# Storing the weight sums of one more feed-forward block, and making the sums in two parts around the latents

## The chip, the core and the metric

The kernel runs on one core of a Trainium2 chip. TensorE (PE) multiplies, VectorE (DVE) and ScalarE (ACT) work element by element, GpSimd (POOL) does small things and starts some transfers, SyncE (SP) starts the others. The metric is the time of one execution in microseconds on the device; the profile's span, from the first to the last instruction, is a little shorter.

## The reference

Two layers run over a stream of 256 tokens of 2048 numbers. Each layer mixes tokens and then applies a gated feed-forward network:

```python
for i in range(DEPTH):                      # 2
    mix = _hybrid_mixer(x, positions, w_in[i], g_cq[i], g_ckv[i], w_uq[i], w_ukv[i], w_o[i])
    x = _layer_norm(ALPHA * x + mix, ln1_g[i], ln1_b[i])
    h = silu(x @ w_gate[i]) * (x @ w_up[i])  # 2048 -> 5632
    x = _layer_norm(ALPHA * x + h @ w_down[i], ln2_g[i], ln2_b[i])
```

The mixer projects `x` with one matrix `w_in`. Its columns give queries, keys and values of sparse attention, an indexer that picks 64 keys for a query, and two latents (`cq`, `ckv`), which are normed by their root mean square and projected again (`w_uq`, `w_ukv`) for latent attention. All is float32.

## The kernel before

**Products in three passes.** A float32 weight tile of 128 x 1024 (a unit: 2 times 128 rows, 512 columns) is loaded as `raw`. ACT copies it to `wh`, rounded to the format that PE multiplies fast (L350), and DVE makes the rest `wl = raw - wh` (L351). `x` is held as a high and a low half too (`xhl`). A product of 128 x 128 by 128 x 512 is three matmuls: high by `wh`, high by `wl`, low by `wh` (L372 to L374, L690 to L692, L993 to L996, L1105 to L1107).

**A layer in order.** `proj` runs over the units of a block of `w_in`; the blocks come as QI0, TA (the indexer's key and weights, and most of `cq`), QI1, TB (the rest of `cq`, and `ckv`), KA0, then the latents' products (`w_uq`, `w_ukv`, in `mla_half` and `nope_T`), QA0, VA0 and so on, and the output projection with `w_o`. Behind TB, `tb_post` norms the latents, with POOL taking the power (L601, L603) and DVE scaling by it (L604). The feed-forward part has 11 blocks fc of 512 columns. Each has a gate and up part, here gu(fc), and hidden activations `hT`, which come in pairs into down parts, here d(fc), the one ahead of gu(fc).

**Quads.** From fc = 1 on gu(fc) goes by a scheme with seven products in place of eight. A quad takes units u and u + 4 of gate and of up for both halves of the tokens. A plain quad (N) has 8 passes over 4 loaded units, each 2 x 3 matmuls. A Strassen-Winograd quad (S) has 7 passes on 7 weight tiles: three are units, four are sums and differences of units that DVE makes on the spot (L1050, L1057, L1062, and a sum by an adding transfer, L329 and L330). It also needs four combinations of `x` for its unit, kept in `many` or `few`, made by `sum_operands` (L932, L937 and `split`). A made quad (Q) is the same with the four weight sums read from device memory, `ready[fc]`, where they were stored during attention. `ORDER` and `UNIT` say which quad runs where: NSSS for fc = 1, SSNS for 2 and 3, and SSQS from `ALLFROM` = 4 on, with unit `EARLY` = 0 for Q.

**Sets.** `presums` makes the stored sums. A set is one fc: four units are loaded on POOL's queue (L778) into `q`, four DVE operations make the sums (L789, L790, L792, L793), four transfers on POOL's queue store them (L798). `not_until_now` (L339) is a one-column POOL operation that writes into the new tile and reads the newest `wh`, so that the load can't start before the work has come so far; `gate` (L788) does the same for the sums. There are four `q` tiles, so that one set follows the other.

**What sets the order.** Side tasks such as `presums`, `indexer` and `mla_attend` are Python generators: `spawn` starts one, `yield n` lets n units of `proj` go by (`tick`), `finish` runs one to its end. That order of writing is the priority by which the framework fills each engine's queue ahead of the run, where it takes a later instruction into a gap if its inputs and a buffer are free. Each engine then works its queue in that order. Tiles with one tag share a fixed number of slots: `a8` has 10 of 8 KB a partition, for the two `x`, the four halves of the split `x`, `few`, `hT` and others, and a tile whose slot is taken waits for the last reader of an older one. `first_operands` makes the combinations for unit 0 in the down part ahead of fc = `ALLFROM`, behind the first column of its first `hT`.

Of the kernel before, what the change touches and what calls it, by code (L numbers as in the profile page):

```python
# [55 lines left out]
NFC = FFN // C  # L56
# [5 lines left out]
SOON = 200  # L62
FIRSTD = 2
T2, T2MORE = 4, 6
ALLFROM, EARLY = 4, 0


QI0, TA, QI1, TB, KA0, QA0, VA0, KA1, QA1, VA1 = range(10)
# [14 lines left out]
def hybrid_trunk(ctx: ExitStack, tc: tile.TileContext, x, xt_in, pos, w_in, g_cq, g_ckv, w_uq,  # L83
# [9 lines left out]
    def nm(s):  # L93
        uid[0] += 1
        return f"{s}{uid[0]}"
# [7 lines left out]
    def turn(name):  # L103
        if phase["cm"] is not None:
            phase["cm"].__exit__(None, None, None)
        phase["cm"] = None
        if name is not None:
            phase["cm"] = tc.tile_pool(name=nm(name), bufs=1)
            phase["pool"] = phase["cm"].__enter__()
        phase["name"] = name  # L110

    def pt(shape, dt, s, tag=None, bufs=1):
        assert phase["name"] == "att"
        return phase["pool"].tile(shape, dt, name=nm(s), tag=tag or s, bufs=bufs)

    def t4(shape, dt, s):
        return pt(shape, dt, s, "a4", 8)
# [33 lines left out]
    def f(ap):  # L151
        return ap.bitcast(F32)
# [22 lines left out]
    def load_x():  # L175
        for t in range(NT):
            nc.sync.dma_start(xt[t], x[t * P:(t + 1) * P, :])
# [105 lines left out]
    def step(task):  # L283
        try:
            task[0] = units_gone[0] + (next(task[1]) or 1)
        except StopIteration:
            tasks.remove(task)
# [7 lines left out]
    def spawn(gen):  # L295
        task = [0, gen]
        tasks.append(task)
        step(task)
        return task
# [5 lines left out]
    def finish(*ends):  # L305
        while any(e in tasks for e in ends):
            for task in list(tasks):
                if any(e in tasks for e in ends):
                    step(task)
# [25 lines left out]
    def not_until_now(*tiles):  # L335


        for v in tiles:
            nc.gpsimd.tensor_tensor(v[:, 0:1], mhalf, f(latest["wh"][:, 0:1]), op=ALU.add)  # L339
# [18 lines left out]
    def proj(units, lhs, n, before=None, split_t=None, banks=None):  # L358

        o = [bank(i, "acc") for i in banks] if banks else [acc() for _ in range(NT)]
        loaded = []
        last = len(units) - 1

        def go(t, u):
            (wh, wl), ks = loaded[u], units[u][1]
            for j, k in enumerate(ks):
                h, l = lhs(t, k)
                a, b = wh[:, j, :n], wl[:, j, :n]  # L370
                first, final = u == 0 and j == 0, u == last and j == len(ks) - 1
                mm(o[t][:, :n], h, a, start=first, stop=False)  # L372
                mm(o[t][:, :n], h, b, start=False, stop=False)  # L373
                mm(o[t][:, :n], l, a, start=False, stop=final)  # L374

        for u, (src, ks) in enumerate(units):
            if before is not None:
                before(u)
            loaded.append(load_unit(src, src.shape[-1]))
            for t in range(1 if split_t else NT):  # L380
                go(t, u)
            tick()
        if split_t:
            split_t()
            for u in range(len(units)):
                go(1, u)
                tick()
        return o
# [149 lines left out]
    def layer(l, xT, norms, last):  # L538
        xk = xlhs(xT)

        def in_chunk(b, before=None, split_t=None):
            n = IN_BLOCKS[b][1]
            return proj([(w_in[b][l, u], range(u * KU, (u + 1) * KU)) for u in range(NKT // KU)], xk, n,
                        before, split_t)
# [191 lines left out]
        def dsa_qk(b):  # L736
            dst = t4([P, 4, S], F32, "qk")
            o = in_chunk(b)
            return dst, spawn(heads_T(o, 4, A_DIM, A_ROT, [cosA[:, t] for t in range(NT)],
                                      [sinA[:, t] for t in range(NT)], dst))  # L740
# [26 lines left out]

        ready = {}

        def presums():  # L770

            for fc in range(ALLFROM, NFC):
                u = EARLY

                def load(i, v):
                    d = pt([P, KU * C], F32, "q", bufs=4)
                    not_until_now(d)
                    nc.gpsimd.dma_start(d, w_gu[i][l, fc, v])  # L778
                    return d

                b12, b22 = load(1, u), load(1, u + HALF)
                yield 1
                b11 = load(0, u)
                yield 1
                b21 = load(0, u + HALF)
                yield 4
                gate = pt([P, 1], F32, "gate", bufs=2)
                nc.gpsimd.tensor_tensor(gate, b12[:, 0:1], f(latest["wh"][:, 0:1]), op=ALU.add)  # L788
                nc.vector.tensor_tensor(b12, b12, b22, op=ALU.add)  # L789
                nc.vector.tensor_tensor(b11, b12, b11, op=ALU.add)  # L790
                yield 1
                nc.vector.tensor_tensor(b22, b11, b22, op=ALU.subtract)  # L792
                nc.vector.tensor_tensor(b21, b11, b21, op=ALU.add)  # L793
                yield 1
                ready[fc] = {}
                for i, (name, v) in enumerate((("p7", b12), ("p6", b11), ("p5", b22), ("p4", b21))):
                    d = hbm.tile([P, KU * C], F32, name=nm("q"), tag=f"{l}_{fc}_{name}", bufs=1)
                    nc.gpsimd.dma_start(d, v)  # L798
                    ready[fc][name] = d
                    if i % 2:  # L800
                        yield 1

        def aff(c):
            if l:
                affine(ln2_g[l - 1], ln2_b[l - 1], c)
# [20 lines left out]
        ckvT = t4([P, 2, KVL // P, S], F32R, "ckvT")  # L826
        qpT = t4([P, M_HEADS // 2, S], F32, "qpT")
        bias = [pt([P, P * (t + 1)], F32, f"selb{t}") for t in range(NT)]
        o = in_chunk(TA)
        aff(1)  # L830
        p_ta = spawn(ta_post(o))
# [6 lines left out]
        p_tb = spawn(tb_post(o))  # L838
        if l == 0:
            load_x()  # L840
        early = spawn(presums())
        ka, p_ka = dsa_qk(KA0)
        finish(p_tb)
        o = proj([(w_uq[2][l, u], range(u * KU, (u + 1) * KU)) for u in range(QL // P // KU)], cqk, C)
# [54 lines left out]
                        nc.vector.scalar_tensor_tensor(sl, o, by, sl, op0=ALU.mult, op1=ALU.add)  # L899
                then(t)  # L900

        finish(early)
        turn("more")
        gbT = load_gbT(ln1_T[l])
        xT, norms = [], []
# [241 lines left out]
        def finish_hidden():  # L1147
            finish(*[h[2] for h in held])

        ORDER = {1: "NSSS", 2: "SSNS", 3: "SSNS"}  # L1150
        UNIT = {"NSSS": (0, 2, 3, 1), "SSNS": (1, 2, 0, 3), "SSQS": (1, 2, EARLY, 3)}

        g = gu(0, 0, lambda: finish(*norms))
# [5 lines left out]
        for fc in range(1, NFC):  # L1159
            order = ORDER.get(fc, "SSQS")  # L1160
            if fc >= FIRSTD:
# [24 lines left out]
    for l in range(DEPTH):  # L1186
        xT, norms = layer(l, xT, norms, l == DEPTH - 1)
# [51 lines left out]
```

## Time and profile before

| | |
|---|---|
| time, median of 3 runs | 2145.45 us |
| lowest and highest | 2143.92 and 2145.48 us |
| time of the profiled execution | 2147.09 us |
| its span | 2145.3 us |
| granted TensorE clock, mean | 0.997 of 2.4 GHz |
| busy: PE, weight loads, DVE, ACT, POOL | 99%, 82%, 86%, 61%, 15% |
| read from and written to device memory | 503.37 MB and 31.46 MB |

Times of rows are counted from the start of the span. The first 20 us are start-up, about 20 to 434.8 us is attention and gate and up of block 0 in layer 0, and layer 1 begins near 1071. Matmuls are pipelined, and a matmul is listed with the time from its start to its modelled end, which overlaps the next. Releasers in brackets say what ended the idle time before an instruction.

### The profile page before, as it was taken

How to read it: one execution, taken by the hardware profiler on the slowest of the kernel's cores; microseconds unless marked ns; L12 is line 12 of the kernel's file. 1: busy time of each engine (PE TensorE's matmuls, PEld its weight loads, DVE VectorE, ACT ScalarE, POOL GpSimd, SP SyncE). 2: the span in 40 equal slices, each digit the busy share in tenths (PEclk: the TensorE clock that was granted, in tenths of full speed). 3: DMA queues.
4: the chain of work that ended last, by engine and by line, in shares of the span. 5: the costliest groups of instructions: out<-in, count | busy, mean ns of one | idle time of the engine just before them, and what ended most of it. 6: DMA issues, size and time to landing. Idle time of an engine off the chain costs nothing.

```text
span 2145.3 us, 28442 instructions
## 1 busy us (share of the span) xinstructions
PE 2129.4 (99%) x9946; PEld 1768.9 (82%) x9946; DVE 1850.9 (86%) x2343; ACT 1311.5 (61%) x1695; POOL 321.6 (15%) x514
## 2 busy tenths in 40 slices
PE   9999999999999999999999999999999999999997
PEld 7888888888888888888888888888888888888886
DVE  6697776899999999999867976678999999999997
ACT  5555554766566666766655555447666666666773
POOL 0122220021111100110013222201111111110111
PEclk9999999999999999999999999999999999999999
DMA  8677879588888899888657877885897888989984
GB/s 295 216 279 272 310 277 328 175 217 267 239 245 270 286 278 300 269 273 255 216 176 242 298 276 276 315 281 187 245 274 224 256 265 274 288 275 293 286 296 115
DMA packets 161905, 558.21 MB, mean 260 GB/s; under 512 B 18161, under 2 KB 18465, under 8 KB 161121
## 3 DMA queue, kind: packets, MB, share of 16 engines
q1 hardware_dynamic: 111168, 399.69, 52.2%
q0 software_dynamic: 50448, 156.57, 28.4%
q8 instruction: 78, 1.28, 0.2%
q14 instruction: 67, 0.54, 0.1%
q10 hardware_dynamic: 144, 0.13, 0.0%
HBM read 503.37 MB, written 31.46 MB: 249 GB/s over the span
## 4 chain that ended last, share of the span: by engine, by line
PE 86%; DVE 7%; issue 3%; DMA 2%; ACT 1%; POOL 0%; SPq 0%; POOLq 0%; DVEq 0%; ACTq 0%
PE acc L372 8%; PE acc L373 8%; PE acc L374 8%; PE acc L1106 7%; PE acc L1107 7%; PE acc L1105 7%; PE gu_p L996 6%; PE gu_p L993 6%; PE gu_p L995 6%; DVE wl L351 3%; PE gu_c L993 3%; PE gu_c L996 3%; PE gu_c L995 3%; PE tr L392 2%; PE att L993 2%
## 5 line engine op out<-in xcount | busy, mean ns | idle before, releaser
L350 ACT ACTIVATE wh<-raw 128x1024 fp32r<-128x1024 f32 (+1 forms) x918 | 946.6, 1053 | 576.0 <-PE acc L374 142.8
L351 DVE TENSOR_TENSOR wl<-raw,wh 128x1024 fp32r<-128x1024 f32 (+1 forms) x918 | 1084.9, 1213 | 204.4 <-ACT wh L350 202.4
L372 PE MATMUL acc<-wh,xhl 128*128 128x512 f32 (+1 forms) x768 | 303.0, 395 | 0.8 <-ACT wh L350 0.7
L373 PE MATMUL acc<-wl,xhl 128*128 128x512 f32 (+1 forms) x768 | 297.2, 387 | 1.1 <-DVE wl L351 1.1
L374 PE MATMUL acc<-wh,xhl 128*128 128x512 f32 (+1 forms) x768 | 297.5, 388 | 0.0
L1105 PE MATMUL acc<-wh,hT 128*128 128x512 f32 x640 | 250.9, 392 | 0.0
L1106 PE MATMUL acc<-wl,hT 128*128 128x512 f32 x640 | 249.2, 389 | 0.1
L1107 PE MATMUL acc<-wh,hT 128*128 128x512 f32 x640 | 249.3, 390 | 0.0
L372 PEld LDWEIGHTS acc<-wh,xhl 128*128 128x128 f32 x768 | 144.7, 188 | 31.9 <-issue 3.9
L373 PEld LDWEIGHTS acc<-wl,xhl 128*128 128x128 f32 x768 | 144.8, 188 | 28.6 <-DVE wl L351 2.9
L374 PEld LDWEIGHTS acc<-wh,xhl 128*128 128x128 f32 x768 | 144.5, 188 | 27.9
L1106 PEld LDWEIGHTS acc<-wl,hT 128*128 128x128 f32 x640 | 120.2, 188 | 25.3 <-DVE wl L351 1.0
L1107 PEld LDWEIGHTS acc<-wh,hT 128*128 128x128 f32 x640 | 120.1, 188 | 25.1
L1105 PEld LDWEIGHTS acc<-wh,hT 128*128 128x128 f32 x640 | 120.2, 188 | 24.3
L1114 POOL DMA_DIRECT2D x<-d x80 | 67.8, 848 | 482.4 <-ACT d L1113 482.1
L995 PE MATMUL gu_c<-wl,xhl 128*128 128x512 f32 x344 | 134.0, 390 | 0.0
L996 PE MATMUL gu_c<-wh,xhl 128*128 128x512 f32 x344 | 133.8, 389 | 0.0
L993 PE MATMUL gu_c<-wh,xhl 128*128 128x512 f32 x344 | 133.8, 389 | 0.0
L993 PE MATMUL gu_p<-wh,many 128*128 128x512 f32 x240 | 93.4, 389 | 0.0
L995 PE MATMUL gu_p<-wl,many 128*128 128x512 f32 x240 | 93.4, 389 | 0.0
L996 PE MATMUL gu_p<-wh,many 128*128 128x512 f32 x240 | 93.4, 389 | 0.0
L1113 ACT ACTIVATE d<-acc 128x512 f32<-128x512 f32 x80 | 47.8, 597 | 71.5 <-PE acc L1107 70.8
(296 smaller groups left out, 3795.8 us busy)
## 6 DMA issues: line engine op xcount, KB each, us to landing
raw<-in_w_gate_dram SPq DMA_DIRECT2D x176, 512.0 KB, 5.4
raw<-in_w_down_dram SPq DMA_DIRECT2D x176, 512.0 KB, 8.6
raw<-in_w_in_dram SPq DMA_DIRECT2D x144, 512.0 KB, 5.2
sum<-in_w_up_dram POOLq DMA_DIRECT2D x120, 512.0 KB, 7.4
raw<-in_w_up_dram SPq DMA_DIRECT2D x102, 512.0 KB, 5.7
raw<-in_w_o_dram SPq DMA_DIRECT2D x64, 512.0 KB, 5.6
q<-q POOLq DMA_DIRECT2D x56, 512.0 KB, 4.4
raw<-q SPq DMA_DIRECT2D x56, 512.0 KB, 5.9
```

What stands on the lines that cost most here:

```text
L350: nc.scalar.activation(wh[:, :n], raw[:, :n], AF.Copy)
L351: nc.vector.tensor_tensor(wl[:, :n], raw[:, :n], f(wh[:, :n]), op=ALU.subtract)
L372: mm(o[t][:, :n], h, a, start=first, stop=False)
L373: mm(o[t][:, :n], h, b, start=False, stop=False)
L374: mm(o[t][:, :n], l, a, start=False, stop=final)
L993: mm(o[name], h, a, start=name not in begun, stop=False)
L995: mm(o[name], h, b, start=False, stop=False)
L996: mm(o[name], l, a, start=False, stop=end)
L1105: mm(o[c][t], h, wh[:, j, :], start=begin, stop=False)
L1106: mm(o[c][t], h, wl[:, j, :], start=False, stop=False)
L1107: mm(o[c][t], lo, wh[:, j, :], start=False, stop=end)
L1114: nc.gpsimd.dma_start(xt[t][:, c * C:(c + 1) * C], d, accum_op=ALU.add)
```

## The change

Block 3 takes the order SSQS in place of SSNS: its plain quad becomes a made quad, and `first_operands` moves one block ahead with `ALLFROM` = 3. A layer stores eight sets in place of seven. `presums` takes the list of its blocks and a number of units to wait for at its start. The sets of blocks 3 and 4 are begun before TA, one unit in. The other six are begun where all seven were, behind TB, but three units later.

```diff
--- before.py
+++ after.py
@@ -62,7 +62,7 @@
 SOON = 200
 FIRSTD = 2
 T2, T2MORE = 4, 6
-ALLFROM, EARLY = 4, 0
+ALLFROM, EARLY = 3, 0
 
 
 QI0, TA, QI1, TB, KA0, QA0, VA0, KA1, QA1, VA1 = range(10)
@@ -767,9 +767,10 @@
 
         ready = {}
 
-        def presums():
-
-            for fc in range(ALLFROM, NFC):
+        def presums(fcs, wait=1):
+
+            yield wait
+            for fc in fcs:
                 u = EARLY
 
                 def load(i, v):
@@ -826,6 +827,7 @@
         ckvT = t4([P, 2, KVL // P, S], F32R, "ckvT")
         qpT = t4([P, M_HEADS // 2, S], F32, "qpT")
         bias = [pt([P, P * (t + 1)], F32, f"selb{t}") for t in range(NT)]
+        early = [spawn(presums([ALLFROM, ALLFROM + 1]))]
         o = in_chunk(TA)
         aff(1)
         p_ta = spawn(ta_post(o))
@@ -838,7 +840,7 @@
         p_tb = spawn(tb_post(o))
         if l == 0:
             load_x()
-        early = spawn(presums())
+        early.append(spawn(presums(range(ALLFROM + 2, NFC), 3)))
         ka, p_ka = dsa_qk(KA0)
         finish(p_tb)
         o = proj([(w_uq[2][l, u], range(u * KU, (u + 1) * KU)) for u in range(QL // P // KU)], cqk, C)
@@ -899,7 +901,7 @@
                         nc.vector.scalar_tensor_tensor(sl, o, by, sl, op0=ALU.mult, op1=ALU.add)
                 then(t)
 
-        finish(early)
+        finish(*early)
         turn("more")
         gbT = load_gbT(ln1_T[l])
         xT, norms = [], []
@@ -1147,7 +1149,7 @@
         def finish_hidden():
             finish(*[h[2] for h in held])
 
-        ORDER = {1: "NSSS", 2: "SSNS", 3: "SSNS"}
+        ORDER = {1: "NSSS", 2: "SSNS"}
         UNIT = {"NSSS": (0, 2, 3, 1), "SSNS": (1, 2, 0, 3), "SSQS": (1, 2, EARLY, 3)}
 
         g = gu(0, 0, lambda: finish(*norms))
```

## Rows read from the trace of the kernel before

**Rows 1.** The page, part 1: busy time, share and instructions of the engines.

```profile
PE 2129.4 (99%) x9946; PEld 1768.9 (82%) x9946; DVE 1850.9 (86%) x2343; ACT 1311.5 (61%) x1695; POOL 321.6 (15%) x514
```

**Rows 2.** Stretches: length, busy us of PE, PEld, DVE, ACT, POOL; clock, DMA share.

```profile
20.00:2145.30 2125.30, 2112.86 (x9885) 1755.70 (x9883) 1838.95 (x2318) 1299.35 (x1674) 316.73 (x454) 1.00 0.81 260
```

**Rows 3.** PE's waits after 20 us: who waited for whom, total, times, longest.

```profile
PE acc L373 <- DVE wl L351: 0.3, 1, 0.3
PE tr L533 <- ACT pr L526: 0.2, 1, 0.2
PE tr L392 <- DVE cqT L396: 0.2, 1, 0.2
```

**Rows 4.** Stretches again: gu(3), gu(4), d(5) of layer 0; gu(3), gu(4) of layer 1.

```profile
560.84:600.28 39.44, 39.44 (x175) 32.66 (x174) 38.16 (x44) 27.79 (x32) 5.04 (x7) 1.00 0.92 266
...
622.97:661.05 38.08, 38.08 (x170) 31.54 (x168) 36.27 (x34) 30.06 (x31) 5.05 (x7) 1.00 0.93 292
661.05:683.70 22.65, 22.65 (x105) 18.85 (x104) 21.64 (x21) 11.45 (x14) 2.51 (x4) 1.00 0.83 252
...
1624.53:1663.97 39.44, 39.44 (x176) 32.67 (x174) 38.17 (x44) 28.22 (x32) 5.34 (x7) 1.00 0.91 264
...
1686.65:1724.73 38.08, 38.08 (x169) 31.53 (x168) 36.19 (x34) 28.52 (x31) 5.23 (x7) 1.00 0.92 291
```

**Rows 5.** PE's timeline where gu(3) begins: start, duration, line, output, operands.

```profile
560.84 0.39 PE L993 MATMUL gu_p<-wh,xhl 128*128 128x512 f32 x1
```

**Rows 6.** Timelines of DVE and PE: low halves made, matmuls that read them.

```profile
657.88 1.21 DVE L351 TENSOR_TENSOR wl<-raw,wh 128x1024 fp32r<-128x1024 f32 x1
...
661.27 0.39 PE L1106 MATMUL acc<-wl,hT 128*128 128x512 f32 x1
...
574.34 5.75 DVE L351 TENSOR_TENSOR wl<-raw,wh 128x1024 fp32r<-128x1024 f32 x5
...
580.11 0.39 PE L995 MATMUL gu_c<-wl,xhl 128*128 128x512 f32 x1
...
1193.93 1.22 DVE L351 TENSOR_TENSOR wl<-raw,wh 128x1024 fp32r<-128x1024 f32 x1
...
1196.84 0.28 PE L692 MATMUL acc<-cqT,wl 128*128 128x256 f32 x1
...
549.74 0.39 PE L1107 MATMUL acc<-wh,hT 128*128 128x512 f32 x1
...
536.87 1.22 DVE L351 TENSOR_TENSOR wl<-raw,wh 128x1024 fp32r<-128x1024 f32 x1
```

**Rows 7.** Groups by line: count, busy us, mean ns, idle before and its ender.

```profile
L351 DVE TENSOR_TENSOR wl<-raw,wh 128x1024 fp32r<-128x1024 f32 (+1 forms) x918 | 1084.9, 1213 | 204.4 <-ACT wh L350 202.4
L350 ACT ACTIVATE wh<-raw 128x1024 fp32r<-128x1024 f32 (+1 forms) x918 | 946.6, 1053 | 576.0 <-PE acc L374 142.8 <-PE acc L1107 95.9 <-issue 72.7
...
L789 DVE TENSOR_TENSOR q<-q,q 128x1024 f32<-128x1024 f32 x14 | 17.1, 1222 | 0.7
```

**Rows 8.** One stretch: TA, QI1 and TB of layer 1.

```profile
1096.00:1163.00 67.00, 67.00 (x348) 57.97 (x347) 43.71 (x90) 32.77 (x46) 15.22 (x22) 1.00 0.82 262
```

**Rows 9.** DVE's timeline: the first sum of the first set in layer 0.

```profile
110.01 1.22 DVE L789 TENSOR_TENSOR q<-q,q 128x1024 f32<-128x1024 f32 x1
```

**Rows 10.** Operands of unit 0: DVE's timeline, and the tile's view in layer 0.

```profile
560.61 0.42 DVE L932 TENSOR_TENSOR av<-xhl 128x256 f32<-128x256 f32 x1
...
L396 DVE TENSOR_TENSOR few<-sv,few x4: 413/416/419, 584.6 to 600.2; 128x256 fp32r<-128x256 f32 x4
```

**Rows 11.** The page, part 3: queue, packets, MB, share of 16 engines.

```profile
q1 hardware_dynamic: 111168, 399.69, 52.2%
q0 software_dynamic: 50448, 156.57, 28.4%
```

**Rows 12.** Line L339 with ns min/median/max; DVE's timeline at the latents' norm.

```profile
L339 POOL TENSOR_TENSOR q<-mhalf,wh x56: 180/918/1569, 85.1 to 1355.2; 128x1 f32<-128x1 f32 x56
...
106.61 0.48 DVE L604 SCALAR_TENSOR_TENSOR rn<-ckv,rrs,gk 128x256 f32<-128x256 f32 x1 [0.72 <-POOL rrs L603]
```

## Prediction

> **What bounds the kernel now.** I read the page's busy line first. TensorE (PE) has work for 99% of the span, VectorE (DVE) for 86% [rows 1], so the second question is whether PE ever waits. After the first 20 us it is busy for 2112.86 of 2125.30 us [rows 2], and the list of its waits in that stretch adds up to 0.7 us, 0.3 + 0.2 + 0.2 [rows 3]; what else is missing is the end, where the last norm runs without matmuls. The third view is the table of stretches: each block of the feed-forward layer, gate and up (gu) or down (d), has PE busy for the whole of its length [rows 4]. The edges are read in PE's timeline: gu(3) of layer 0 begins with the first L993 behind an L1107, at 560.84 [rows 5], and it ends where the next L1105 starts, which is the other edge of its stretch, 600.28; the others are read likewise. So the kernel is bound by the number of its matmuls, and a matmul taken away is worth its pitch. A matmul is listed with 0.39 us, but they overlap: 174 fill 39.44 us, and that is 0.2267 us each.
>
> The fourth thing to read is how far DVE is ahead, since it makes the low halves (`wl`) that PE reads. I pair the end of a `wl` with the first matmul that reads it. Ahead of d(5), where a block with a made quad ends, the `wl` is ready at 657.88 + 1.21 = 659.09 and read at 661.27: 2.2 us [rows 6]. Ahead of the third quad of gu(3) the second of five is ready at about 576.7 and read at 580.11: 3.4 us [rows 6]. In the latents' block the second unit of the first key and query product is ready at 1195.15 and read at 1196.84: 1.7 us [rows 6]. These are the reserves that every addition to DVE has to be set against.
>
> **The change part by part.** *Fewer matmuls.* A plain quad is 8 passes, a made one 7, and a pass is 2 x 3 matmuls: 48 become 42, in one block, in two layers. 6 x 0.2267 x 2 = 2.72 us. The profile has the same number as a difference of rows: gu(3), with its plain quad, takes 39.44, gu(4), with the made one, 38.08, and in layer 1 1624.53 to 1663.97 against 1686.65 to 1724.73 gives the same 39.44 and 38.08 [rows 4]. 2 x 1.36 = 2.72.
>
> *More halves.* The made quad loads 7 raw tiles where the plain one loads 4. Each of the 3 more takes 1.05 on ACT and 1.21 on DVE [rows 7]: 3.2 and 3.6 us a layer. They lie beside PE, and gu(4) shows how it fits: 36.27 of 38.08 us of DVE [rows 4], and PE does not wait. I cost them at nothing; what hides them is the 2.2 us that DVE is ahead at the end of such a block, and block 3 would then look as block 4 does now.
>
> *The sums.* A set is 4 DVE operations of 1.22 us [rows 7], 4.9 us, and 8 transfers of 512 KB on POOL's queue. One set more per layer. Two sets now come under the blocks TA, QI1 and TB, where in layer 1 DVE has 43.71 us of work in 67 [rows 8]: 9.8 more fits. The six others begin three units later than the seven did. In layer 0 the first set's first sum stands at 110.01 [rows 9]; three units of 12 matmuls later is 8.2 us later, and that brings it to the end of KA0, close to the latents' products. So 4.9 us leave DVE's queue ahead of the place with 1.7 us of reserve, and 4.9 us enter it right at that place. Bounds: nothing, if the total ahead of it counts, and 4.9 - 1.7 = 3.2 us a layer, if DVE can't use the room that was made. I take nothing, since DVE's order is kept by the program's order and the sum ahead of the product is the same; the upper end is kept for the range.
>
> *The operands of unit 0.* `first_operands` moves from d(4) to d(3): 12 small DVE operations of 0.42 us [rows 10], 5.0 us, and 4 copies on ACT. Now they are spread over the slack of the plain quad in gu(3), from 560.61 to about 600 [rows 10], a block ahead of their place. That slack goes away. Block 3 with its down block would have 36.27 + 21.64 + 5.0 = 62.9 us of DVE in 38.08 + 22.65 = 60.73 of PE [rows 4]: 2.2 too much, against a reserve of 2.2. Bounds: nothing and 5.0 - 2.2 = 2.8 us a layer. I take nothing, because the row at 560.61 shows these operations taken early into gaps, and gu(2) with its plain quad has such a gap.
>
> *A slot.* All ten `a8` slots are held in d(3): 2 of `x`, 4 of the split `x`, 1 `few`, 3 of `hT`. So the second `few` waits for the `hT` of block 0, whose last matmul starts at 549.74 [rows 6]. Behind that wait stand, on ACT's queue, the next weights' high halves, and behind these DVE. It costs nothing where the copy stands behind these in the queue; its upper end is the rival below.
>
> *Transfers.* In layer 1 from 1096 to 1163 the DMA engines are busy to 0.82 [rows 8]. Two sets are 8 MB, of which 2 MB of loads lie there already. By the page 156.57 MB on queue 0 took 28.4% of the span, 3.9 us for a MB [rows 11], so 6 MB are 23 us, and 0.82 x 67 + 23 = 78 us do not fit in 67. At the 2.8 us that 399.69 MB in 52.2% on queue 1 give [rows 11], it is 72, or 5 over. What is late need not be a weight; bounds nothing and 5 us, in layer 1 alone. I take nothing, since gu(4) runs at a share of 0.93 without a wait [rows 4].
>
> *POOL.* Eight more of the one-column POOL operations that hold a load back. They take from 180 ns to 1569, median 918 [rows 12]: a 180 ns operation that is mostly held by something. The six sets' holds now fall among the POOL operations of the latents' norm, for which DVE waits in its order, 0.72 us at one of them [rows 12]. The Trainium skill (SBUF — State Buffer, section "Who interferes with whom") says that a DVE instruction with two SBUF inputs and a GpSimd instruction that reads SBUF exclude each other, and that the later one waits for the whole of the first. By that rule the longer ones are those that met a `wl`, and the trace agrees, since 1.22 is a `wl`'s length. What it makes of the time is the third rival.
>
> Sum: the profiled execution has a span of 2145.3 us and a time of 2147.09, 1.6 above the median of the three runs shown, 2145.45. The span becomes 2142.6, and the median 2145.45 - 2.72 = 2142.7.
>
> **The rivals.**
> *DVE's reserve is spent* on the operands or on the sums beside the latents. For it: 62.9 against 60.73, and 1.7 us. Against it: PE waits nowhere now in spite of a DVE at 95% in gu(4). The full price is 2 x (2.8 + 3.2) = 12.0; a third of it, 4.0 us, is what I would expect: 2146.7.
> *Late transfers* in layer 1: 2142.7 + 4.7 = 2147.4. Against it: one stretch, and queued weights are asked for early.
> *POOL holds the norm up*: four of its operations each start later by one DVE operation of 1.21 [rows 7], 4.8 us, less the reserve of 1.7, in two layers: 6.2, so 2148.9. Against it: the norm's operations meet such holds already.
> *Slower, by the slot.* If ACT's copy into the second `few` stands right behind the fourth unit of d(3), whose low half is ready at 538.09 [rows 6], ACT stands from 538.1 until 550.1 and DVE with it: 12.0 us. DVE has 2.8 us of gaps in a block with its down part (60.73 - 57.91 [rows 4]) and the reserve of 3.4, so 12.0 + 5.0 - 2.8 - 3.4 = 10.8 us a layer reach PE: 2142.7 + 21.6 = 2164.3. It decides from a wait of 4.7 us on: then 2 x (4.7 - 1.2) = 7.0 is lost, and the gain of 2.72 turns into a loss of 4.3. Against it: the queue's order is made ahead by the framework, which knows of the slot.
> *The change does less than it says*: the made quad waits for its stored sums or for `few`. Both are made over 100 us and at least 20 us ahead of their use; I give that no chance of its own.
>
> **How the numbers follow.** 0.2% is 4.3 us, about what a measurement of this kernel can tell from no change. Forecast 2142.7, chance 0.68, with the scatter of the three runs about 2141.0 to 2144.3. Reserve spent 0.14, late transfers 0.06, POOL 0.04, the slot 0.05. The remaining 0.03 is for a gain that I can't name: the waits that are left to win, 0.7 us, do not reach 4.3. The range from 2141.0 to 2147.4 takes in the forecast, late transfers, and the smaller two thirds of the spent reserve, 0.82 or so. Faster by over 0.2%: 0.06 (the unnamed gain and a little scatter). Slower by over 0.2%: 0.08 (the slot, and the upper end of POOL's and the reserve's). Within: 0.86.
>
> **What the profile would show.** Right: gu(3) at 38.08 us in both layers, 12 matmuls fewer, 6 `wl` from raw tiles more, 8 stores of `q` more, two sets' sums before 100 us, and no new wait in PE's list. Wrong: PE waiting for `wl` at the latents' products (reserve or POOL), in d(3) or gu(3) (slot: an ACT copy into `few` with an idle time before it that a matmul on `hT` ended), or for `wl` in TA to TB of layer 1 behind a late raw tile. What would make the forecast wrong above all is the order in which the queues are filled, of which the trace of before shows only one instance.

## The result: slower by 17 us

The changed kernel takes 2162.34 us (median of six runs, 2159.05 to 2164.12) against 2144.94 of the kernel before (six runs, 2143.92 to 2146.22): a ratio of 1.0078, with a 95% interval from 1.0065 to 1.0091. The forecast was 2142.7 with a range up to 2147.4. The profiled execution of after took 2162.73, with a span of 2161.0.

The first view is again the table of stretches of after (columns as in [rows 2]): everything behind the first 20 us, gu(3) of layer 0, gu(3) of layer 1, and TA to TB of layer 1.

```profile
20.00:2161.00 2141.00, 2112.87 (x9860) 1754.02 (x9859) 1855.05 (x2329) 1301.27 (x1677) 327.12 (x480) 0.99 0.81 263
564.85:602.93 38.08, 38.08 (x169) 31.53 (x168) 36.19 (x34) 28.74 (x31) 5.22 (x7) 1.00 0.92 291
1641.42:1679.50 38.08, 38.08 (x170) 31.53 (x168) 35.52 (x33) 29.49 (x31) 5.23 (x7) 1.00 0.93 286
1096.00:1163.00 67.00, 59.87 (x281) 50.15 (x280) 39.48 (x69) 24.65 (x33) 22.11 (x38) 0.95 0.90 306
```

gu(3) is at 38.08 us in both layers, where it was 39.44 [rows 4]: the gain is there. But PE is idle for 2141.00 - 2112.87 = 28.13 us behind the first 20, where it was 12.44 [rows 2]; the 15.7 us more are the whole difference of the spans (2161.0 - 2145.3). The busy time did not fall by the quad's 2.7 us, since a lowered clock, shown below, stretches other matmuls. And in layer 1 a stretch of 67 us that had no idle time [rows 8] now has 7.13. PE's waits after 20 us, the whole list, against 0.7 us in [rows 3]:

```profile
PE tr L392 <- DVE dup L574: 9.8, 2, 5.6
PE att L651 <- ACT rel L656: 3.2, 2, 1.8
PE acc L373 <- DVE wl L351: 1.6, 1, 1.6
PE tr L533 <- ACT pr L526: 1.1, 2, 0.6
PE tr L392 <- DVE cqT L396: 0.3, 1, 0.3
PE tr L392 <- ACT kpT L582: 0.2, 1, 0.2
```

They add up to 16.2, 15.5 more than before. Two of them are 9.8 us: the two transposes of TA's small tiles (`dup`, from which `kiT` is made), in layer 0 at 58 us and in layer 1 at 1129 us. Nothing of that is near the quad, whose blocks begin at 564.85 and 1641.42 us. The timeline of ACT, DVE and PE of after shows how the wait of layer 0 comes about (start, duration, line, output and operands, and in brackets the idle time before and who ended it):

```profile
53.05 1.06 ACT L350 ACTIVATE wh<-raw 128x1024 fp32r<-128x1024 f32 x1 [4.76 <-DMA raw<-in_w_in_dram]
55.49 0.22 ACT L572 ACTIVATE dup<-acc 128x64 f32<-128x64 f32 x1 [1.38 <-DVE wi L587]
59.22 1.06 ACT L350 ACTIVATE wh<-raw 128x1024 fp32r<-128x1024 f32 x1 [3.51 <-DMA raw<-in_w_in_dram]
...
60.59 0.22 ACT L572 ACTIVATE dup<-acc 128x64 f32<-128x64 f32 x1
...
60.31 1.23 DVE L351 TENSOR_TENSOR wl<-raw,wh 128x1024 fp32r<-128x1024 f32 x1 [3.74 <-ACT wh L350]
...
62.07 0.20 DVE L574 COPY dup<-dup 128x64 f32<-128x64 f32 x1
...
62.41 0.45 PE L392 MATMUL tr<-ident,dup 128*128 128x128 f32 x1 [4.22 <-DVE dup L574]
```

Read it from below. PE's second transpose waits 4.22 us for the second `dup` (62.07), which comes from ACT's copy at 60.59. That copy has 0.22 us of work; it stands in ACT's order behind a halving (59.22) that waits 3.51 us for a weight tile to land, and DVE's part behind the low half of the same tile. The late thing is a transfer, and it is a transfer of layer 0. The stall of layer 1 ends in the same way, behind a halving that waits for a weight:

```profile
1131.24 1.06 ACT L350 ACTIVATE wh<-raw 128x1024 fp32r<-128x1024 f32 x1 [4.33 <-DMA raw<-in_w_in_dram]
...
1134.43 0.45 PE L392 MATMUL tr<-ident,dup 128*128 128x128 f32 x1 [5.57 <-DVE dup L574]
```

What the DMA engines carry from 40 to 60 us in layer 0, first in before, then in after (share of the 16 engines by queue; KB each and median us from issue to landing):

```profile
q1 hardware_dynamic: 1464, 6.32, 86.0%
...
raw<-in_w_in_dram SPq DMA_DIRECT2D x6, 512.0 KB, 5.0
x<-in_x_dram SPq DMA_DIRECT2D x2, 1024.0 KB, 7.2
```

```profile
q1 hardware_dynamic: 1119, 5.14, 68.9%
q0 software_dynamic: 580, 2.12, 26.0%
...
raw<-in_w_in_dram SPq DMA_DIRECT2D x6, 512.0 KB, 11.5
x<-in_x_dram SPq DMA_DIRECT2D x2, 1024.0 KB, 10.8
q<-q POOLq DMA_DIRECT2D x4, 512.0 KB, 13.0
q<-in_w_up_dram POOLq DMA_DIRECT2D x2, 512.0 KB, 8.4
```

A weight lands after 11.5 us (median) in place of 5.0. What is new there is the first set's stores (`q<-q`) and the second set's loads; they meet the 2 MB of `x`, which SP's queue asks for between the weights. Whether that is the cause the experiments test. The clock adds to it. Of two stretches of after, the stall and what follows, the seventh number is the granted clock:

```profile
58.00:62.00 4.00, 0.19 (x2) 0.00 (x0) 1.66 (x6) 1.92 (x4) 1.36 (x4) 0.84 1.03 423
63.00:67.30 4.30, 4.30 (x11) 3.30 (x10) 2.20 (x2) 1.53 (x4) 0.00 (x0) 0.50 1.03 420
```

Behind the stall PE runs at 0.50, which is 1.2 GHz: ten matmuls 0.427 us apart, against 0.2267 at 2.4 GHz, 2.0 us lost. The same follows the 5.6 us in layer 1, where the clock is at 0.50 from 1134.5 to 1139 us.

### The profile page after: what moved, and what is told of

Its sections match the earlier page's. It is cut to its first block, busy times and chain, and to the rows that moved or that the text cites. A ratio compares the mean times of both kernels' runs of the same rounds, so it can differ in the third digit from the quotient of the medians.

```text
span 2161.0 us, 28509 instructions
## 1 busy us (share of the span) xinstructions
PE 2130.3 (99%) x9934; PEld 1768.5 (82%) x9934; DVE 1868.1 (86%) x2357; ACT 1315.1 (61%) x1701; POOL 332.0 (15%) x540
## 4 chain that ended last, share of the span: by engine, by line
PE 81%; DVE 8%; issue 5%; DMA 4%; ACT 1%; POOL 1%; POOLq 0%; SPq 0%; DVEq 0%; ACTq 0%
PE acc L372 7%; PE acc L373 7%; PE acc L374 7%; PE acc L1108 7%; PE acc L1109 7%; PE acc L1107 7%; PE gu_p L997 6%; PE gu_p L998 6%; PE gu_p L995 6%; DVE wl L351 4%; PE gu_c L998 3%; PE gu_c L997 3%; PE gu_c L995 3%; PE tr L392 2%; DMA raw<-in_w_in_dram 2%
## 5 line engine op out<-in xcount | busy, mean ns | idle before, releaser
L998 PE MATMUL gu_c<-wh,xhl 128*128 128x512 f32 x336 | 130.7, 389 | 0.0
L995 PE MATMUL gu_c<-wh,xhl 128*128 128x512 f32 x336 | 130.7, 389 | 0.0
L329 POOL DMA_DIRECT2D sum<-in_w_up_dram x60 | 33.3, 555 | 445.8 <-DVE wl L351 415.3
L995 PE MATMUL gu_p<-wh,many 128*128 128x512 f32 x240 | 93.4, 389 | 0.0
```

Of the source, the lines that this page charges most:

```text
L995: mm(o[name], h, a, start=name not in begun, stop=False)
L998: mm(o[name], l, a, start=False, stop=end)
```

## The experiments

The theory (T): the early sets' transfers crowd out weights that are wanted in TA to TB, and ACT's and DVE's order turns late weights into PE's waits. Rivals: the sums' work on DVE (V), and the quad itself with its slot, operands and reserves (Q).

### Which part of the change it is

**split_alone** keeps the kernel before's quads and makes the sets as the change does:

```
-ALLFROM, EARLY = 3, 0
+ALLFROM, EARLY = 4, 0
...
-        ORDER = {1: "NSSS", 2: "SSNS"}
+        ORDER = {1: "NSSS", 2: "SSNS", 3: "SSNS"}
```

> The kernel before with its quads and its seven sets, but two of these begun ahead of TA and five behind TB with the pause of three units. Transfers: the whole loss of the change without its gain, 2162.3 + 2.7 = 2165. VectorE: the same, since the sums are there too; this run tells only whether the split makes the loss. If the quad or the operands made it: some 2145.

Measured: 2165.3 us, ratio 1.0096 (1.0082 to 1.0110), with a wait list that begins like that of after (9.4 us on `dup`). **quad_only** is the other half: before's seven sets, and block 3 with block 4's sums. (Where a pause of 0 units is given, here and below, `presums` skips its first `yield`; that line is left out of the cuts.)

```
-        early = [spawn(presums([ALLFROM, ALLFROM + 1]))]
-        early.append(spawn(presums(range(ALLFROM + 2, NFC), 3)))
+        early = [spawn(presums(range(ALLFROM + 1, NFC), 0))]
...
+        ready[ALLFROM] = ready[ALLFROM + 1]
```

> Block 3's quad by itself: the kernel before's seven sets, begun behind TB as there, and block 3 computed as in after, with block 4's stored sums for its own, so that block 3's set is not made at all (its result is left wrong thereby). If the matmul term of the sum is right and the slot, the few operands and the reserves cost nothing: 12 matmuls of 0.2267 us less, 2142.3 +- 0.5, with gu(3) at 38.08 us in both layers. If the quad brings a cost that the traces so far hide under the other losses: 2144 or more.

Measured: 2141.94 us against 2145.05, ratio 0.9986 (0.9978 to 0.9995). gu(3) takes 38.09 and 38.08, and this is the whole of PE's wait list:

```profile
PE tr L392 <- DVE cqT L396: 0.2, 1, 0.2
```

So Q falls, and with it the slot, the operands of unit 0 and the reserve at the end of d(3): the quad brings what the matmuls say, and the loss of 2162.3 - 2141.9 = 20.4 us is made by the sets alone (one more of them, and their new places).

### Sums or transfers

**no_early_sums** leaves out the two early sets' sums, **no_early_stores** their stores:

```
-                nc.vector.tensor_tensor(b12, b12, b22, op=ALU.add)
-                nc.vector.tensor_tensor(b11, b12, b11, op=ALU.add)
+                if sums:
+                    nc.vector.tensor_tensor(b12, b12, b22, op=ALU.add)
+                    nc.vector.tensor_tensor(b11, b12, b11, op=ALU.add)
...
+                if not store:
+                    yield 1
+                    yield 1
+                    continue
```

> The changed kernel without the eight VectorE operations of the two early sets in each layer: their tiles are loaded and stored as they are, so that the output is not the reference's. All transfers stay. Transfers: the loss stays, 2158 to 2163, with PE waiting some 10 us in all for the tile dup. VectorE: the loss goes, 2142 to 2146.

> The changed kernel without the eight stores of the two early sets in each layer; blocks 3 and 4 read the sums of blocks 5 and 6, so that the output is not the reference's. 4 of the 8 MB a layer are gone, the sums on VectorE stay. Transfers: most of the loss goes, 2143 to 2150. VectorE: it stays, 2158 to 2163.

Measured: 2165.35 us (1.0092, 1.0077 to 1.0107) without the sums, where nothing is won (it is 2 us above the range written down), and 2149.64 (1.0026, 1.0016 to 1.0035) without the stores, where 12.7 of the 17.4 us go. V falls. What the second leaves is, above all, one wait for `dup`, 4.6 us, in layer 1: there the loads are enough, beside what layer 1 carries anyway.

### No set ahead of TA

**all_behind** begins all eight sets behind TB:

```
-        early = [spawn(presums([ALLFROM, ALLFROM + 1]))]
...
-        early.append(spawn(presums(range(ALLFROM + 2, NFC), 3)))
+        early = [spawn(presums(range(ALLFROM, NFC), 0))]
```

> The changed kernel with all eight sets begun behind TB, with no pause, where the kernel before begins its seven. Theory of transfers (the two early sets fill the DMA engines between TA and TB, raw weight tiles land late, and ACT, in its order, waits for them with the work of TA behind it): the loss goes and the seven-pass quad's gain stays, 2.7 us under the kernel before, some 2142.5, with 38.08 us for gu(3) and no wait of PE for the tile dup. Theory of VectorE (the sums stand in its queue ahead of the low halves): the eighth set costs what a set costs there, so about 2145 to 2150. If the quad itself, or the operands of unit 0, were the loss, it stays at some 2160.

Measured: 2152.67 us, ratio 1.0036 (1.0023 to 1.0048); 10 us worse than T said. TA to TB is clean, but there is a wait that no theory had:

```profile
PE acc L895 <- DVE x L873: 6.8, 2, 4.0
```

It lies at the last pass of the product with `w_o`, once a layer, while the gate weights are asked for. The eighth set itself is through by then, its last store is issued at 340.40 us; but on POOL's queue it pushes back the first `sum` transfers of the quads, which now fall on the gate weights. The first pair, in before and in all_behind:

```profile
322.01 1.06 POOL L329 DMA_DIRECT2D sum<-in_w_up_dram  x2 [7.18 <-ACT oA L395]
```

```profile
349.11 1.06 POOL L329 DMA_DIRECT2D sum<-in_w_up_dram  x2 [8.17 <-issue]
```

The adding halves follow at 330.07 and 332.62 us in before, at 356.78 and 359.33 in all_behind. From 355 to 370 us a gate weight lands after 4.3 us in before and after 13.9 in all_behind (medians). ACT's timeline there:

```profile
366.81 1.06 ACT L350 ACTIVATE wh<-raw 128x1024 fp32r<-128x1024 f32 x1 [2.87 <-DMA raw<-in_w_gate_dram]
369.99 2.23 ACT L350 ACTIVATE wh<-raw 128x1024 fp32r<-128x1024 f32 x2 [2.12 <-DMA raw<-in_w_gate_dram]
```

It is the same figure in another place: a halving waits for a tile, and DVE's `x` stands behind the low half. **short_pace** is all_behind with sets of 9 units in place of 10, so that the eight end earlier:

```
                 b21 = load(0, u + HALF)
-                yield 4
+                yield 3
```

> All eight sets begin behind TB without a pause, as in all_behind, but each takes 9 units in place of 10 (the sums come 3 units after the last load, not 4), so that they end after 72 units, where the seven sets of the kernel before ended after 70, and not after 80. The transfer theory, widened by all_behind's last pass (what counts is which piece of PE's work lies under the crowd of transfers): neither TA-TB nor the pass with w_o meets a crowd that the kernel before did not have, PE waits under 1 us after 20 us, and the quad's 2.7 us remain as gain: 2142 to 2143.5. Rival, that eight sets are too many transfers for the attention stage wherever they lie: 2148 to 2156, with waits in other places.

Measured: 2149.63 us, ratio 1.0018 (1.0009 to 1.0028). The `sum` transfers start at 331.81 us and the wait at the last pass falls to 0.7 us, but 3.4 us come up in the attention (`PE tr L533 <- ACT pr L526`). The rival is the nearer: in these two paces eight sets behind TB are paid for in one place or the other.

### What the early sets meet

**x_held** holds back the load of `x` in layer 0:

```
         if l == 0:
+            not_until_now(*xt)
             load_x()
```

> The kernel after, but in layer 0 the 2 MB load of x may start only when TB's weights are there (in after it is issued at 40.5 and 44.2 us, amid the loads and stores of the early sets); layer 1 has no such load. If the transfers' crowd at 40 to 60 us makes layer 0's stall, taking 2 MB out of it takes away most of the 4.2 us wait and the 2 us of lowered clock: 2155 to 2158, with layer 1's waits unchanged. If the early sets' own transfers do it alone: 2161 to 2163.

Measured: 2156.80 us, ratio 1.0052 (1.0037 to 1.0067), 5.5 us less than after. From 20 to 1000 us PE now waits once, 0.6 us; what is left on `dup` is layer 1's:

```profile
PE tr L392 <- DVE dup L574: 6.4, 1, 6.4
```

**affine_late** takes the four pieces of the gain and shift out of QI0 to QI1 of layer 1 (`aff(0)` to `aff(3)` now begin at VA0, KA1, QA1 and VA1):

```
-        aff(1)
         p_ta = spawn(ta_post(o))
-        aff(2)
...
         m = mla_half(1)
+        aff(1)
         ka, p_ka = dsa_qk(KA1)
...
+        aff(2)
         qa, p_qa = dsa_qk(QA1)
```

> The kernel after, but the four pieces of layer 1's second normalisation's gain and shift (a broadcast load of 256 KB and two accumulating ones each, on POOL's queue, with two products on VectorE) are begun at VA0, KA1, QA1 and VA1 instead of around QI0 to QI1; layer 0 is as in after. If they are what the early sets meet in layer 1: of layer 1's 13.6 us (waits of 1.6, 5.6, 1.8 and 1.4 us, 0.8 us at the attention, 2 us of lowered clock) over half goes, layer 0 keeps its 6.4 us: 2150 to 2156. If the early sets crowd out the weights by themselves: 2160 to 2164, with the wait at TA's transposes still over 4 us.

Measured: 2149.46 us, ratio 1.0019 (1.0010 to 1.0028), 12.9 us less than after. That is half a microsecond below the range written down. Layer 1's waits are gone from the list but for 0.4 us, and its 6.0 us on `dup` are layer 0's (4.2 in after, whose layer 0 is written the same, so the size of a stall is not fixed). The edit moves three things at once, the pieces' transfers, their products on DVE and their places in POOL's order; no run takes them apart. **early_layer1_only** parts the layers in the other way, **one_ahead** halves the dose:

```
-        early = [spawn(presums([ALLFROM, ALLFROM + 1]))]
+        early = [spawn(presums([ALLFROM, ALLFROM + 1]))] if l else []
...
-        early.append(spawn(presums(range(ALLFROM + 2, NFC), 3)))
+        early.append(spawn(presums(range(ALLFROM + 2, NFC), 3) if l else presums(range(ALLFROM, NFC), 0)))
```

```
-        early = [spawn(presums([ALLFROM, ALLFROM + 1]))]
+        early = [spawn(presums([ALLFROM]))]
...
-        early.append(spawn(presums(range(ALLFROM + 2, NFC), 3)))
+        early.append(spawn(presums(range(ALLFROM + 1, NFC), 0)))
```

> The kernel after in layer 1; in layer 0 all eight sets begin behind TB without a pause, as in all_behind. It parts the loss by layers. From the traces: layer 1 of after is 13.7 us longer in the stretch from QI0 to wuq, layer 0 of all_behind 3.6 us longer in the pass with w_o, the quads give 2.7 us back: 2145 + 13.7 + 3.6 - 2.7 = about 2159.5. If layers did not add up (the loss of one depends on what the other left), the time would be off that by over 3 us.

> The kernel after with one early set (block 3's) in place of two; the other seven begin behind TB without a pause, as in the kernel before. The dose of the crowd at TA is halved: 4 MB a layer instead of 8. In layer 0 the second set's loads of after fell on QI1, the first set's stores on the load of x at 40 to 47 us, which is still there: the wait at TA's transposes stays at 1 to 4 us; in layer 1 the first set meets the affine pieces: the wait shrinks by half. By the transfer theory 2145 to 2154; if the loss came from the second set alone, 2142 to 2143; if one set is enough for the whole, 2160.

Measured: 2162.82 (1.0077, 1.0062 to 1.0092) and 2158.59 us (1.0062, 1.0050 to 1.0075). The first is 3.3 above the sum that was written down, just over the 3 us that were to mean that the layers do not add up; some 2 us of it are the lowered clock behind layer 0's wait of 3.6 us (0.50 from 372 to 377 us), which the sum had left out. The second is a miss: half the transfers make four fifths of the loss (16.6 of the 20.4 us above quad_only). The waits at TA are nearly those of two sets, 3.5 us (layer 0) and 5.2 us (layer 1, here put down to ACT's `cq`); what the second set adds are the waits on `rel` and `pr` behind it. The loss is not proportional to the bytes.

### How late weights become PE's wait

**dup_later** changes no transfer, but transposes TA's tiles two units later:

```
                 nc.scalar.activation(cq[t][:, 0:432], o[t][:, 80:512], AF.Copy)
-            yield 2
+            yield 4
```

> The kernel after, but the two transposes of TA's small tiles (kiT) come 4 units behind TA instead of 2; the transfers stay as they are. In the trace of after PE waits there 4.2 us (layer 0) and 5.6 us (layer 1), because the copies that feed the transposes stand in ACT's and DVE's order behind halvings that wait for weights; the weights that PE wants next came 0.9 us and some 2.2 us late if PE had gone on without the transposes. If the order on ACT and DVE is what turns late transfers into these stalls: the dup wait disappears, waits on wl of 1 to 3 us a layer come in its place, the clock stays up in layer 0 and the time is 2151 to 2158. If PE is short of weights anyway, the stall only changes its name (wl for dup) and the time stays within 2 us of 2162.

Measured: 2160.95 us, ratio 1.0068 (1.0053 to 1.0083): only 1.4 us less than after, as the rival said. Its list begins

```profile
PE acc L373 <- DVE wl L351: 5.6, 2, 4.3
PE att L651 <- ACT rel L656: 5.4, 3, 2.6
PE tr L392 <- DVE dup L574: 1.8, 2, 1.4
```

Layer 0 loses its stall at TA, as the order said (0.35 us is left there), but two waits on `rel` come behind; layer 1 only changes the name, 4.3 us on `wl` at 1144 us. So the order decides who is seen waiting; with the order changed, the late weights cost nearly the same.

### Is there a place for the transfers?

**one_ahead_xheld** and **one_later_xheld** hold `x` back as in x_held and begin one set ahead of TA, or ahead of QI1 (the cut is of the second), and the other seven behind TB without a pause:

```
         aff(2)
+        early = [spawn(presums([ALLFROM]))]
         o = in_chunk(QI1)
```

> As one_ahead, and in layer 0 the load of x is held back till TB's weights are there. In x_held, with two early sets, layer 0 had no wait at all left at TA, so with one it has none: layer 0 gains its 1.4 us of the quad, and what is lost is layer 1's alone, 0 to 6 us: 2142 to 2149. Should the seven sets then meet the held load of x behind TB: waits at wuq or the attention in layer 0, over 2149.

> As one_ahead_xheld, but the early set begins one projection later, ahead of QI1 instead of ahead of TA, where the kernel before's mean DMA share was 0.5 to 0.6 in layer 0 (56 to 86 us) and 0.54 in layer 1 (1136 to 1146 us). If it is the place of the transfers that decides, and not their number: no wait at TA's transposes in either layer, 2142 to 2145, level with or faster than the kernel before. If any eighth set costs what it brings, as all_behind and short_pace suggest (2149 to 2153): 2146 to 2152.

Measured: 2155.65 (1.0053, 1.0040 to 1.0065), beyond its first range, and 2148.07 (1.0011, 1.0002 to 1.0020). Both get new waits on `rel` at about 100 to 110 us, behind the held `x`, which is asked for at 83.6 and 83.3 us and lands within 12.2 us; from 85 to 110 us the weights take 12.7 and 11.4 us (medians) to land, against 8.8 in x_held; the first keeps layer 1's stall of 5.5 us, the second has only small ones there. **both_late** is after with everything that the early sets met moved away: the gain and shift as in affine_late, and the halves of `x` ahead of KA1 and QA1. **one_later_both_late** has the same moves with one set ahead of QI1 and seven behind TB, **before_both_late** the same moves in the kernel before.

```
-        if l == 0:
-            load_x()
...
+        aff(1)
+        if l == 0:
+            not_until_now(xt[0])
+            load_x([0])
         ka, p_ka = dsa_qk(KA1)
...
+        aff(2)
+        if l == 0:
+            not_until_now(xt[1])
+            load_x([1])
         qa, p_qa = dsa_qk(QA1)
```

> As affine_late, and in layer 0 the two halves of x are loaded ahead of KA1 and QA1 instead of behind TB (held until then). If x and the pieces of the gain and shift are together the whole of what the early sets meet between TA and TB: neither layer waits over 1 us there and the quad's 2.7 us come through, 2142 to 2146 (more, if the moved transfers make new waits in the attention). If the early sets make waits by themselves: 2150 or more.

> One early set that begins ahead of QI1, seven behind TB without a pause, x and the gain and shift moved as in both_late. one_later_xheld lost 3.9 us in layer 0 (the held x load behind TB) and some 3 us in layer 1; if those are the moved transfers' doing, both go: 2141.5 to 2143.5, ahead of the kernel before by the quad. If an eighth set has a price wherever it lies: 2145 to 2149.

> The kernel before with x's load and the gain and shift pieces moved as in both_late, and nothing else. PE waited 0.7 us in all after 20 us in the kernel before, so there is nothing for the move to win: 2145 +- 1, or up to 4.5 us more if the piece at QA1 makes the same stall here as in both_late (2.3 us and some 2 us of lowered clock). If the moves are worth something by themselves, and the quad nothing: 2143 or less.

Measured: 2143.18 us, ratio 0.9991 (0.9982 to 0.9999); 2147.67, ratio 1.0009 (1.0000 to 1.0018); 2150.03, ratio 1.0024 (1.0015 to 1.0033). The first is the changed kernel at work: both early sets, no stall at TA in either layer. It is the only version with an eighth set that is ahead of the kernel before, by 2.0 us with an interval that ends at 0.9999, so barely. The second misses its first range and lies in that of its rival: it has no stall at TA either, but a wait of 2.9 us on `qk` near 1315 us and two of 0.3 and less; what else sets it 4.5 us behind both_late is open. The third is at the upper end of its range, with a wait of 3.6 us on `qk` at the same place. It shows that the moves by themselves win nothing: they cost 5 us where seven sets lie behind TB. It is the exchange of places that pays. The wait list of both_late and, for the two places of the stall, its stretches, with that of after from 40 to 60 us behind them:

```profile
PE tr L392 <- ACT qk L550: 2.1, 1, 2.1
PE acc L373 <- DVE wl L351: 0.3, 1, 0.3
```

```profile
1096.00:1163.00 67.00, 67.00 (x350) 57.49 (x349) 48.64 (x98) 34.77 (x55) 19.91 (x32) 1.00 0.86 311
40.00:60.00 20.00, 20.00 (x91) 16.50 (x89) 14.78 (x26) 10.28 (x16) 8.18 (x12) 1.00 0.98 382
```

```profile
40.00:60.00 20.00, 18.19 (x81) 14.78 (x79) 11.53 (x18) 6.86 (x9) 4.54 (x11) 1.00 0.95 364
```

In both places both_late moves more per second than after (306 GB/s in the first, in the table at the top; 364 in the second), and PE is busy throughout. **both_late_gain_first** was to take away the 2.1 us, where DVE stands 5.57 us before a product with a gain piece:

```
+        aff_load(0)
         va = dsa_v(VA0)
         aff(0)
+        aff_load(1)
...
```

> both_late, but each gain piece's load is issued one projection ahead of the products that need it. In both_late VectorE stood 5.57 us before the products at 1305.07 us, waiting for the load, with a weight's subtraction, the softmax's work and so the transposes on PE behind it. If that is the stall: it and its lowered clock go, 4 us, against up to 0.5 us for the loads elsewhere: 2139.5 to 2142, level with or ahead of the quad by itself. If it is the crowd of transfers at 1290 to 1310 us at large: the stall stays and the time is that of both_late, 2143.

Measured: 2146.42 us, ratio 1.0007 (0.9998 to 1.0016): no gain, and 3.2 us more than both_late. The edit did not do what it was for: POOL issued the load at 1295.50 us, where both_late had issued it at 1294.53, and DVE waited 6.55 us for it. Whether that load is the cause stays open.

## Why the prediction was wrong

*The matmuls: right.* 39.44 became 38.08 us twice, and quad_only has the 2.7 us, 3.1 by its medians.

*Halves, operands, slot: right at nothing.* quad_only has them all, and a wait of 0.2 us. The rival of 2164.3 came within 2 us of the measured time by luck: its mechanism is absent, since PE waits nowhere in d(3) or gu(3).

*The sums and POOL: right at nothing*, as far as the sums are DVE's work. The reserve beside the latents was not spent: of the list of after, 0.5 us (`cqT`, `kpT`) belong to the latents' block, against 0.2 in [rows 3].

*Transfers: this is the step that failed.* "I take nothing, since gu(4) runs at a share of 0.93 without a wait", with an upper bound of "5 us, in layer 1 alone". Measured by taking away what the sets meet: 12.9 us in layer 1 (affine_late) and 5.5 us in layer 0 (x_held), 19.2 together (both_late). These are differences of whole kernels and hold what the moved work costs in its new place, too. Three things were wrong in it.

First, layer 0 was left out. The load of `x` is a transfer of 2 MB in the very stretch into which the sets were moved, and its stretch was not read: from 45 to 55 us the kernel before already had a DMA share of 0.96.

```profile
45.00:55.00 10.00, 10.00 (x46) 8.29 (x45) 4.75 (x4) 3.92 (x4) 0.00 (x0) 1.00 0.96 371
```

Second, a mean share was taken for a measure of room, both for the bound (78 us of work in 67) and against it (0.93 in gu(4)). It measures neither: at 0.86 and 311 GB/s both_late has no wait, at 0.90 and 306 after has 7 us; at 0.98 against 0.95 the same once more. How long a weight of 512 KB takes to land goes better with the loss. From 40 to 60 us the medians are 5.0, 6.7, 8.3 and 11.5 us in before, both_late, x_held and after, and only after stalls. From 1096 to 1130 us they are 6.5 in before, 6.4 in both_late, 5.9 in affine_late and 8.1 in after, and again only after stalls. But it is no threshold either, since 8.3 us cost x_held nothing in layer 0 and 8.1 went with a stall of 5.6 us in layer 1. In both_late the engines are about as full as in after, and yet its weights come in time.

The price of a MB was wrong as well, and not in the way that would have helped: the sets take 2.5 us a MB (last section) where the prediction used 3.9, and with 2.5 its own overflow of 11 us shrinks to 3 (an estimate, 0.82 x 67 + 6 x 2.5 - 67).

Third, the price was an overflow, so many us too much in a stretch. What PE pays is decided by who stands behind the late tile in ACT's and DVE's order, and a small copy that two transposes need stood there. So the sign to look for ("PE waiting for `wl`") was nearly the wrong one: 1.6 of the 16.2 us have that name. On top came 2.0 us of lowered clock behind each large stall, which no term had.

The rival "late transfers" had the mechanism and the layer, with a chance of 0.06 and 4.7 us; it had 4.7 of the 12.9 us of layer 1, and none of layer 0.

The Trainium skill (DMA: Bandwidth & Descriptors, section "Queues, rings and completion order") states that each DMA engine takes turns between the queues that have work, packet by packet. The trace agrees as far as it goes: with sets on POOL's queue the weights' queue falls from 86.0 to 68.9% of the engines from 40 to 60 us; the turns themselves are in no view here. Why the pieces of the gain weigh so heavily no run here parts further; what the rows say of it stands in the last section.

## What to carry over

Before transfers are moved, read, in every layer, how long the weights take to land in the stretch that they move to and how long PE could do without them, and list what else is asked for there; a mean share of the DMA engines says neither that there is room nor that there is none. Then follow each in-order queue behind a weight's first use: the wait will bear the name of what stands last in it. And if a change loses where its own gain is plainly in the trace, look for the neighbour that it met: moving that one away turned 17 us of loss into 2 us of gain, though the same move by itself costs 5.

## What was not expected of the hardware

The pieces of the gain and shift hold the DMA engines longer per byte than weights or sets do. From 1096 to 1130 us of the kernel before, queue 0 carries nothing but these pieces; the same stretch of both_late carries sets on it:

```profile
q1 hardware_dynamic: 1752, 6.10, 50.6%
q0 software_dynamic: 995, 2.17, 30.3%
```

```profile
q1 hardware_dynamic: 1872, 6.24, 49.8%
q0 software_dynamic: 1616, 5.89, 42.9%
```

2.17 MB in 30.3% of 34 us are 4.7 us for a MB; the sets take 0.429 x 34 / 5.89 = 2.5, the weights 0.506 x 34 / 6.10 = 2.8. The lines give part of the reason: 2.17 MB in 995 packets are 2.2 KB a packet, 5.89 MB in 1616 are 3.6 KB, and a packet holds an engine for about as long in either (0.303 x 34 x 16 / 995 = 0.17 us against 0.14). The 3.9 us of the page's mean over queue 0 [rows 11], which the prediction used for the sets, is made mostly by other transfers: sets are 112 x 512 KB, 58.7 of the 156.57 MB. In gu(4) of layer 0, 622.97 to 661.05 us, queue 0 of the kernel before carries no sets, only the quads' `sum` and the additions of the down parts to `x`, and takes 0.356 x 38.08 / 3.19 = 4.2 us for a MB:

```profile
q0 software_dynamic: 1045, 3.19, 35.6%
```

Among these, as among the pieces, are transfers that add to what is there (`sum` from L330, the shift from L454); no run here sets an adding transfer against a plain one.

The clock's price cannot be read off a wait alone: behind PE's wait of 2.1 us in both_late (1313 us) it was granted at 0.5, behind one of 2.60 us in split_alone (1174 us) it stayed at 1.00:

```profile
1313.30:1316.50 3.20, 3.20 (x13) 2.56 (x11) 3.17 (x4) 1.78 (x4) 0.59 (x1) 0.50 0.87 300
```

```profile
1174.60:1180.00 5.40, 5.40 (x30) 4.65 (x31) 5.01 (x15) 4.81 (x11) 3.96 (x9) 1.00 0.76 270
```
